# Two output-projection blocks begun in turn, and one step more ahead of a product, in a two-layer decoder trunk

## The chip, the core and the metric

The kernel runs on one core of a Trainium2 chip. The metric is device time in microseconds (us) of one execution, the median of three runs. The engines are named as in the profile: PE (TensorE, matmuls; PEld is its weight load), DVE (VectorE), ACT (ScalarE), POOL (GpSimd) and SP (SyncE, which here only issues DMAs).

## The reference

Two layers of a decoder trunk on one sequence of 256 tokens of width 2048, in float32. Each layer projects the normalised input to all heads at once, runs four groups of heads of width 512, gates each, and projects back onto the residual:

```python
h = rms_norm(x, norm_g)
p = split_columns(jnp.einsum("bsd,de->bse", h, w_in))
fox  = from_heads(forgetting_attention(...)) * jax.nn.silu(p["fox_g"])
diff = from_heads(rms_norm(differential_attention(...), diff_norm_g) * (1 - lambda_init)) * silu(p["diff_g"])
moba = from_heads(moba_attention(mq, mk, mv)) * jax.nn.silu(p["moba_g"])
gla  = from_heads(rms_norm(gla_chunked(...), gla_norm_g)) * jax.nn.silu(p["gla_g"])
mixed = jnp.concatenate([fox, diff, moba, gla], axis=-1)
return x + jnp.einsum("bse,ed->bsd", mixed, w_out)
```

With 256 tokens MoBA's blocks of 256 keys leave plain causal attention. After the second layer follows one more RMSNorm.

## The kernel before

**Matmuls.** Nearly all of PE's work is the two projections. For accuracy each weight and each activation is split into two fp32r parts, and three products are added: hi weights with the activation's high part, hi weights with its low part, lo weights with its high part. ACT makes `hi` from the loaded weights (`raw`), DVE makes `lo` as `raw - hi`. The activations, transposed, lie in `hTp` (the layer's normalised input, both parts) and in `mTh` and `mTl` (the mixed heads, high and low part), by k tiles of 128 rows. Four k tiles are a group, which for `mTh`/`mTl` is the output of one kind of heads: 0 forgetting, 1 differential, 2 MoBA, 3 linear attention.

**Steps.** `_blocks()` lists column blocks of `w_in` and `w_out`, `_steps()` cuts them into steps of two k tiles (four, where a block has some 260 columns) and sets their order; the weights lie in memory in that order. A block of 512 columns has eight steps of twelve matmuls (eight with hi, four with lo), which all add into one PSUM tile of the pool `mm` (two buffers). Blocks follow one another, except those with a `turn`: their steps alternate, a group of k tiles of each at a time. Before, only two or three blocks at the start of each layer's `w_in` had one. `w_out` has four blocks of 512 columns in each layer (the last cut in two in layer 1), and takes the groups in the order 3, 0, 1, 2, so that MoBA's is needed last.

**Order of the work.** The program is written out by a loop over the steps, in the order in which every engine then runs its part. For step i it emits: `hi` and `lo` of step i + 3 and the load of step i + 7 (`prepare`); what a finished block leaves to do (`settle`); the step's matmuls (`multiply`), for which the step's groups must have been emitted (`need`); and one round of `tick()`. Everything else, attention, linear attention, the next layer's input, is written as Python generators in the list `tasks`, and each round advances each of them to its next `yield`. So a `yield` is one step of distance. Where `need` isn't met, rounds are run without steps in between.

**The places that the change touches.**
- MoBA ends with `attend_columns`: PE makes p*v (`side<-pT,four`), DVE multiplies by the gate (`four<-side,gate`), `split_group` makes `mTh` on ACT and `mTl` on DVE.
- When a block of `w_out` is finished, `residual` puts it onto `xs` (ACT or DVE) and, in layer 0, starts `make_hT` for the chunk: for chunks 0 and 1 POOL adds x by DMA (L440); DVE transposes 32 x 32 squares (`four<-xs`); `moved` sends the tile to memory (L301, `turn<-four`) and, once that has landed, back in four DMAs in another order (L304, `four<-turn`); after `LAND` = 5 rounds `split_x` makes `hTp` on ACT and DVE. All of POOL's DMAs are issued in one order. Chunk 3 alone is transposed on PE (L281, `side<-ct,xs`).
- In `gla`, for each of two pairs of heads, ACT and DVE make the tile `ee` (`eight` in the profile) and `tq`; a `yield` stands between the last of that and the products of seven levels on PE (`side<-tq,eight`), which take both `side` tiles in PSUM.

Of the kernel before, what the change touches and what calls it, by code (L numbers as in the profile page):

```python
# [24 lines left out]
DEPTH = 2  # L25
# [70 lines left out]
def _blocks():  # L96

    def block(w, l, c0, n, kind, groups=(0, 1, 2, 3), turn=None):
        kts = [g * 4 + i for g in groups for i in range(4)]
        return {"w": w, "l": l, "c0": c0, "n": n, "kind": kind, "kts": kts, "per": 4 if n * 4 <= STEP_W else 2, "turn": turn}  # L100

    out = []
    for l in range(DEPTH):
        for i, (c0, n) in enumerate((
            (COL["gla_a"], 264),
            (COL["gla_q"], 512),
            (COL["gla_g"] + 248, 264),
            (COL["gla_v"], 512),
            (COL["fox_v"] + 258, 258),
            (COL["fox_q"], 512),  # L110
            (COL["fox_k"], 512),
            (COL["diff_q"], 512),
            (COL["diff_k"], 512),
            (COL["fox_v"], 258),
            (COL["fox_g"], 512),
            (COL["diff_v"], 512),
            (COL["moba_q"], 512),
            (COL["moba_k"], 512),
            (COL["diff_g"], 512),
            (COL["moba_g"], 512),  # L120
            (COL["moba_v"], 512),
        )):
            out.append(block("w_in", l, c0, n, "rows", turn=l if i in ((0, 1, 2), (0, 2))[l] else None))
        for chunk in range(4):
            cut = l + 1 == DEPTH and chunk == 3
            out.append(block("w_out", l, chunk * 512, 256 if cut else 512, "rows", (3, 0, 1, 2)))
    out.append(block("w_out", DEPTH - 1, D - 256, 256, "apart", (3, 0, 1, 2)))
    return out


def _steps():

    steps, first = [], {}
    for i, b in enumerate(_blocks()):
        per, turn = b["per"], b["turn"]
        for j in range(0, KT, per):
            key = (i, 0, 0) if turn is None else (first.setdefault(turn, i), j // 4, i)
            steps.append((key, len(steps), {"block": i, "kts": b["kts"][j:j + per], "first": j == 0, "last": j + per == KT}))
    steps = [s for _, _, s in sorted(steps, key=lambda z: z[:2])]
    at = 0  # L140
    for s in steps:
        s["at"] = at
        at += P * len(s["kts"]) * _BLOCKS[s["block"]]["n"]
    return steps
# [61 lines left out]
def hybrid_trunk(  # L206
# [405 lines left out]
    def gla(l, an):  # L612
        yield from until("constants")
        yield
        ps = yield from take_side()
        for m in range(2):
            transpose(ps[0:16, m * P:(m + 1) * P], an[:, m])
        yield
        v_.tensor_copy(at17[0:16], ps[0:16, 0:256])
        side.put(ps)  # L620
        yield
        al = yield from take_side()
        for pair in range(2):
            matmul(al[:, pair * SEQ:(pair + 1) * SEQ], wa[:, l, pair * P:(pair + 1) * P], at17, True, True)
        yield
        e = yield from s2.take([P, 512])
        gl = yield from s2.take([P, 2, SEQ])
        yield from log_sigmoid(gl.rearrange("p x t -> p (x t)"), al[:, :512], e)
        s2.put(e)
        side.put(al)  # L630
        yield
        cum = yield from s2.take([P, 2, SEQ])
        for pair in range(2):
            for m in range(2):
                c = slice(m * P, (m + 1) * P)
                v_.tensor_tensor_scan(cum[:, pair, c], gl[:, pair, c], gl[:, pair, c], 0.0, op0=OP.add, op1=OP.bypass)
        s2.put(gl)
        yield from until(("gla_qk", l))
        qkT = env["gla_qk", l].rearrange("p (a m) t -> p a (m t)", m=2)
        sT = yield from s4.take([P, 2, H, P])  # L640
        for m in range(2):
            for h in range(H):
                c = (h // 2 * 2 + m) * 2 + h % 2
                a_.activation(sT[:, m, h], ident, AF.Copy, scale=env["gla_dgs", l][:, c:c + 1])
            yield
        sx = yield from s2.take([P, H, P])
        for pair in range(2):
            ee = yield from s8.take([P, 2, NL + 1, P])
            for i, h in enumerate(GLA_LEVELS):
                src = cum[:, pair].rearrange("p (m b w) -> p m b w", m=2, w=2 * h)  # L650
                v_.tensor_sub(ee[:, :, i].rearrange("p m (b w) -> p m b w", w=2 * h), src,
                              src[:, :, :, h - 1:h].to_broadcast([P, 2, 64 // h, 2 * h]))
                if i == 3:
                    yield
            v_.tensor_scalar(ee[:, 0, NL], cum[:, pair, :P], cum[:, pair, P - 1:P], None, op0=OP.subtract)
            v_.tensor_copy(ee[:, 1, NL], cum[:, pair, P:])
            yield
            for m in range(2):
                a_.activation(ee[:, m], ee[:, m], AF.Abs)
                a_.activation(ee[:, m], ee[:, m], AF.Exp, scale=-1.0 / GLA_TAU)  # L660
                yield

            def half(z, h, second):
                return z.rearrange("p m (b two h) -> p m b two h", two=2, h=h)[:, :, :, second]

            qv = qkT[:, pair].rearrange("p (m t) -> p m t", m=2)
            kv = qkT[:, 2 + pair].rearrange("p (m t) -> p m t", m=2)
            for i, h in enumerate(GLA_LEVELS):
                for hh in range(2):
                    rows = slice(hh * 64, hh * 64 + 64)  # L670
                    v_.tensor_mul(tq[rows, :, i, hh].rearrange("p m (b h) -> p m b h", h=h), half(ee[rows, :, i], h, 1),
                                  half(qv[rows], h, 1))
                if i == 3:
                    yield
            yield
            for i, h in enumerate(GLA_LEVELS):
                dst = half(ee[:, :, i], h, 0)
                v_.tensor_mul(dst, dst, half(kv, h, 0))
            yield
            v_.tensor_mul(ee[:, 0, NL], ee[:, 0, NL], kv[:, 0])  # L680
            v_.tensor_mul(ee[:, 1, NL], ee[:, 1, NL], qv[:, 1])
            yield
            both = yield from take_both()
            pcs = [z.rearrange("p (l x c) -> p l x c", l=NL + 1, x=2) for z in both]
            for m in range(2):
                for i in range(NL):
                    matmul(pcs[m][:, i], ee[:, m, i], tq[:, m, i], True, True)
            for m in range(2):
                yield
                for i, h in enumerate(GLA_LEVELS):  # L690
                    dst = sT[:, m, pair * 2:pair * 2 + 2].rearrange("p x (b two h) -> p x b two h", two=2, h=h)[:, :, :, 1]
                    src = pcs[m][:, i].rearrange("p x (b h) -> p x b h", h=h)
                    mk = masks[:, i].rearrange("p (b h) -> p b h", h=h)[:, None].to_broadcast([P, 2, 64 // h, h])
                    v_.copy_predicated(dst, mk, src)
                side.put(both[m])
            px = yield from take_side()
            for hh in range(2):
                rows = slice(hh * 64, hh * 64 + 64)
                matmul(px[:, hh * 512:hh * 512 + P], ee[rows, 0, NL], ee[rows, 1, NL], True, True, tiles=2)
            s8.put(ee)  # L700
            yield
            a_.activation(sx[:, pair * 2:pair * 2 + 2], px.rearrange("p (h t) -> p h t", h=2)[:, :, :P], AF.Copy)
            side.put(px)
        s4.put(env["gla_qk", l])
        s2.put(cum)
        yield from until(("gla_v", l))
        yield
        vn = env["gla_v", l]
        ops = yield from take_side()
        o = ops.rearrange("p (m h d) -> p m h d", m=2, h=H)  # L710
        for h in range(H):
            matmul(o[:, 0, h], sT[:, 0, h], vn[:, 0, h * P:(h + 1) * P], True, True)
        for h in range(H):
            matmul(o[:, 1, h], sT[:, 1, h], vn[:, 1, h * P:(h + 1) * P], True, False)
            matmul(o[:, 1, h], sx[:, h], vn[:, 0, h * P:(h + 1) * P], False, True)
        s4.put(sT, vn)
        s2.put(sx)
        yield
        yield from finish_rows(l, 3, o, ops, None, env["gla_sg", l])
# [373 lines left out]
    for z in _BLOCKS:  # L1093
        l, f = next(dones)
# [233 lines left out]
```

## Time and profile before

| what | us |
|---|---|
| median of 3 runs (lowest to highest) | 926.46 (926.28 to 927.83) |
| the profiled execution | 925.78 |
| its span, first to last instruction | 924.0 |
| PE busy | 907.0 |
| DVE busy | 625.6 |
| ACT busy | 506.4 |
| POOL busy | 88.9 |
| mean granted clock of PE, share of full speed | 0.994 |

The profile is of one execution. A row of the timeline gives start and duration in us from the span's start, engine, line of the kernel, operation, what is written and read, and in brackets how long the engine was idle before and what ended that. Line 176 is a helper through which all of ACT's and DVE's work goes, and line 277 one for matmuls, so the tiles' names tell the place. Matmuls overlap in the pipeline: one of 512 columns is shown with 0.39 us while they follow each other faster than that. Each layer has its own rows: layer 0's `w_out` lies about from 365 to 460 us, layer 1's at the end.

### The profile page before, as it was taken

What the parts mean: (1) busy time and instruction counts of PE and PEld (TensorE: products, weight loads), DVE (VectorE), ACT (ScalarE), POOL (GpSimd) and SP (SyncE); (2) the same over time, 40 slices, a digit from 0 to 9 for tenths busy, and PEclk for the clock granted to TensorE, in tenths of its full rate; (3) what the DMA queues carried; (4) which work ended last, traced back from release to release, by engine and by line L of the source; (5) the groups of instructions that cost most, each with busy time, mean ns of one, the idle gap of its engine ahead of it and who ended that gap; (6) DMA issues with size and microseconds to landing.
All of it is one profiled execution on the core that took longest, in us unless ns stands there. A gap on an engine that the chain in (4) does not pass through costs nothing.

```text
span 924.0 us, 12695 instructions
## 1 busy us (share of the span) xinstructions
PE 907.0 (98%) x4694; PEld 771.5 (83%) x4694; DVE 625.6 (68%) x967; ACT 506.4 (55%) x712; POOL 88.9 (10%) x145
## 2 busy tenths in 40 slices
PE   9999999999999999899999999999999999998996
PEld 7989888898888888788898887888888888887886
DVE  7656777787569578556755549867975885694562
ACT  6576773374554466346656575743645545743441
POOL 1010002220001121001200100012110012110000
PEclk9999999999999999999999999999999999999999
DMA  8776557767657768578855845867776576694652
GB/s 320 245 241 190 182 176 260 248 204 229 209 177 230 228 189 235 170 202 261 289 178 164 256 150 178 242 190 247 225 232 178 167 243 207 203 290 147 201 160 92
DMA packets 56865, 194.84 MB, mean 211 GB/s; under 512 B 8001, under 2 KB 8289, under 8 KB 56802
## 3 DMA queue, kind: packets, MB, share of 16 engines
q1 hardware_dynamic: 46048, 164.20, 55.6%
q0 software_dynamic: 9264, 28.32, 10.8%
q10 hardware_dynamic: 1490, 1.51, 0.6%
q8 instruction: 37, 0.61, 0.3%
q14 instruction: 26, 0.21, 0.1%
HBM read 178.79 MB, written 15.20 MB: 210 GB/s over the span
## 4 chain that ended last, share of the span: by engine, by line
PE 95%; DVE 2%; ACT 1%; issue 1%; DMA 0%; POOLq 0%; POOL 0%; DVEq 0%; SPq 0%; ACTq 0%
PE mm L277 86%; PE side L277 9%; ACT eight L176 0%; DMA four<-in_xt 0%; DVE tq L176 0%; DVE lo L176 0%; ACT hi L176 0%; DVE mTl L176 0%; DVE four L176 0%; ACT mTh L176 0%; DVE xs L176 0%; ACT L176 0%; PE side L281 0%; DVE hTp L176 0%; POOLq L1324 0%
## 5 line engine op out<-in xcount | busy, mean ns | idle before, releaser
L176 DVE TENSOR_TENSOR lo<-raw,hi 128x1024 fp32r<-128x1024 f32 (+3 forms) x301 | 364.6, 1220 | 251.8 <-ACT hi L176 250.3
L176 ACT ACTIVATE hi<-raw 128x1024 fp32r<-128x1024 f32 (+3 forms) x301 | 317.1, 1059 | 362.3 <-PE mm L277 310.0
L277 PE MATMUL mm<-hi,hTp 128*128 128x512 f32 (+2 forms) x2048 | 465.1, 371 | 0.0
L277 PEld LDWEIGHTS mm<-hi,hTp 128*128 128x128 f32 x2048 | 358.3, 188 | 66.0 <-ACT hi L176 1.0
L277 PE MATMUL mm<-lo,hTp 128*128 128x512 f32 (+2 forms) x1024 | 249.8, 369 | 0.1
L277 PEld LDWEIGHTS mm<-lo,hTp 128*128 128x128 f32 x1024 | 181.1, 188 | 32.8 <-DVE lo L176 0.3
L277 PE MATMUL mm<-hi,mTh 128*128 128x512 f32 (+1 forms) x256 | 96.7, 382 | 4.8 <-ACT mTh L176 4.8
L277 PE MATMUL mm<-hi,mTl 128*128 128x512 f32 (+1 forms) x256 | 97.0, 383 | 1.5 <-DVE mTl L176 1.5
L277 PE MATMUL mm<-lo,mTh 128*128 128x512 f32 (+1 forms) x256 | 64.4, 376 | 0.0
L277 PEld LDWEIGHTS mm<-hi,mTh 128*128 128x128 f32 x256 | 49.0, 192 | 14.0 <-ACT mTh L176 5.2
L277 PEld LDWEIGHTS mm<-hi,mTl 128*128 128x128 f32 x256 | 49.2, 192 | 11.2 <-DVE mTl L176 2.1
L304 POOL DMA_DIRECT2D four<-turn x84 | 46.0, 553 | 102.2 <-DMA turn<-four 43.5
L277 PEld LDWEIGHTS mm<-lo,mTh 128*128 128x128 f32 x256 | 46.4, 189 | 8.9
L301 POOL DMA_DIRECT2D turn<-four x21 | 12.2, 582 | 407.9 <-DVE four L176 407.9
L176 DVE STREAM_TRANSPOSE pT<-four 32x128 f32<-32x128 f32 (+1 forms) x116 | 39.3, 350 | 1.0
L176 ACT ACTIVATE four<-mm,rstd 128x512 f32<-128x512 f32 (+2 forms) x56 | 33.6, 648 | 3.6 <-DVE fx L176 3.6
L176 ACT ACT_TABLE_LOAD x24 | 30.8, 1283 | 3.3 <-DVE an L176 3.0
L277 PEld LDWEIGHTS side<-four,four 128*128 128x128 f32 (+1 forms) x224 | 22.0, 190 | 2.3 <-issue 1.4
L277 PE MATMUL side<-four,four 128*128 128x128 f32 (+1 forms) x224 | 23.3, 277 | 0.0
L176 DVE STREAM_TRANSPOSE four<-four 128x1024 f32<-128x1024 f32 x18 | 22.4, 1245 | 0.3
L176 ACT ACTIVATE four<-side,nb 128x256 f32<-128x256 f32 (+1 forms) x48 | 20.5, 444 | 0.6 <-DVE nb L176 0.6
L176 DVE COPY_PREDICATED four<-masks,side 128x128 f32<-128x128 uint8 x56 | 19.0, 340 | 1.8
(145 smaller groups left out, 545.1 us busy)
## 6 DMA issues: line engine op xcount, KB each, us to landing
raw<-in_weights SPq DMA_DIRECT2D x272, 512.0 KB, 4.1
turn<-four POOLq DMA_DIRECT2D x21, 512.0 KB, 5.0
four<-turn POOLq DMA_DIRECT2D x84, 128.0 KB, 4.4
raw<-in_weights SPq DMA_DIRECT2D x16, 516.0 KB, 4.9
raw<-in_weights SPq DMA_DIRECT2D x15, 528.0 KB, 4.9
turn<-gate POOLq DMA_DIRECT2D x4, 512.0 KB, 4.8
gate<-turn POOLq DMA_DIRECT2D x16, 128.0 KB, 5.3
four<-in_xt SPq DMA_DIRECT2D x3, 512.0 KB, 7.1
```

The source lines that it names most:

```text
L176: return f(*args, **kw)
L277: t_.matmul(out, lhsT, rhs, start=start, stop=stop)
L301: g_.dma_start(via, t.rearrange("p c a b -> p c (a b)"))
L304: g_.dma_start(t[c * 32:(c + 1) * 32].rearrange("p q a b -> p q (a b)"), via[:, c].rearrange("(q i) e -> i q e", q=4))
```

## The change

```diff
@@ _blocks
-            out.append(block("w_in", l, c0, n, "rows", turn=l if i in ((0, 1, 2), (0, 2))[l] else None))
+            out.append(block("w_in", l, c0, n, "rows", turn=(l, (4, 8, 12)) if i in ((0, 1, 2), (0, 2))[l] else None))
         for chunk in range(4):
             cut = l + 1 == DEPTH and chunk == 3
-            out.append(block("w_out", l, chunk * 512, 256 if cut else 512, "rows", (3, 0, 1, 2)))
+            out.append(block("w_out", l, chunk * 512, 256 if cut else 512, "rows", (3, 0, 1, 2),
+                             turn=(DEPTH + l, (12,)) if chunk < 2 else None))
@@ _steps
-            key = (i, 0, 0) if turn is None else (first.setdefault(turn, i), j // 4, i)
+            key = (i, 0, 0) if turn is None else (first.setdefault(turn[0], i), sum(j >= c for c in turn[1]), i)
@@ gla, for each pair of heads
             v_.tensor_mul(ee[:, 0, NL], ee[:, 0, NL], kv[:, 0])
             v_.tensor_mul(ee[:, 1, NL], ee[:, 1, NL], qv[:, 1])
             yield
+            yield
             both = yield from take_both()
```

A turn now names the k tiles at which it passes to the next block. For `w_in` nothing changes by that. In `w_out` of each layer blocks 0 and 1 form a turn that passes at k tile 12 alone: six steps of block 0, six of block 1, then the last two of block 0 and the last two of block 1. MoBA's group is therefore needed first by the thirteenth step of `w_out` instead of the seventh, block 0 is finished after step 14 instead of 8, block 1 after 16 as before. In `gla` one more `yield` stands ahead of the products of the levels. The number of instructions of the computation stays.

ACT in `w_out` of layer 0, before, from MoBA's `mTh` to the first chunks of the next layer's input (`xs<-mm` copies a finished block, `two,parts<-xs` takes squares of a chunk, `hTp` is the chunk's transposed input):

```order
L176 ACTIVATE four_3312<-mm,rstd 128x512 x2
L176 ACTIVATE hi<-raw 128x1024 x6
L176 ACTIVATE mTh<-four_3442 128x1024
L176 ACTIVATE hi<-raw 128x1024 x2
L176 ACTIVATE xs<-mm 128x512 x2
L176 ACTIVATE hi<-raw 128x1024 x6
L176 ACTIVATE two_3610,parts<-xs 128x512
L176 ACTIVATE two_3612,parts<-xs 128x512
L176 ACTIVATE hi<-raw 128x1024 x2
L176 ACTIVATE xs<-mm 128x512 x2
L176 ACTIVATE hi<-raw 128x1024 x4
L176 ACTIVATE hTp<-four_3607,ngt 128x256 x4
```

And after:

```order
L177 ACTIVATE four_3312<-mm,rstd 128x512 x2
L177 ACTIVATE hi<-raw 128x1024 x9
L177 ACTIVATE mTh<-four_3491 128x1024
L177 ACTIVATE hi<-raw 128x1024 x5
L177 ACTIVATE xs<-mm 128x512 x2
L177 ACTIVATE hi<-raw 128x1024 x2
L177 ACTIVATE xs<-mm 128x512 x2
L177 ACTIVATE hi<-raw 128x1024 x4
L177 ACTIVATE two_3722,parts<-xs 128x512
L177 ACTIVATE two_3724,parts<-xs 128x512
```

`mTh` stands three steps later, block 0's copy six steps later, and block 1's copy comes two steps behind it instead of eight.

POOL between the layers, before (three chunks, each with its way through memory; x is added to chunks 0 and 1):

```order
L440 DMA xs<-in_x 128x2x512
L301 DMA turn_3614<-four_3607 128x1024
L304 DMA four_3607<-turn_3614 32x4x256 x4
L440 DMA xs<-in_x 128x2x512
L301 DMA turn_3783<-four_3776 128x1024
L304 DMA four_3776<-turn_3783 32x4x256 x4
L301 DMA turn_3853<-four_3846 128x1024
L304 DMA four_3846<-turn_3853 32x4x256 x4
```

And after:

```order
L441 DMA xs<-in_x 128x2x512 x2
L302 DMA turn_3726<-four_3719 128x1024
L305 DMA four_3719<-turn_3726 32x4x256 x4
L302 DMA turn_3775<-four_3768 128x1024
L305 DMA four_3768<-turn_3775 32x4x256 x4
L302 DMA turn_3845<-four_3838 128x1024
L305 DMA four_3838<-turn_3845 32x4x256 x4
```

Both additions of x now stand ahead of chunk 0's way through memory, and the three ways follow one another.

PE at the first pair's products of the levels in layer 1, before (`hi` and `lo` carry the number of the step's tile):

```order
L277 MATMUL mm_4739<-lo_4831,hTp_113 128x512 x4
L277 MATMUL side0_4917<-tq_94,eight0_4722 128x128 x7
L277 MATMUL side1_4918<-tq_94,eight0_4722 128x128 x7
L277 MATMUL mm_4946<-hi_4854,hTp_113 128x512 x8
L277 MATMUL mm_4946<-lo_4855,hTp_113 128x512 x4
```

And after:

```order
L278 MATMUL mm_4739<-lo_4831,hTp_113 128x512 x4
L278 MATMUL mm_4930<-hi_4854,hTp_113 128x512 x8
L278 MATMUL mm_4930<-lo_4855,hTp_113 128x512 x4
L278 MATMUL side0_4943<-tq_94,eight0_4722 128x128 x7
L278 MATMUL side1_4944<-tq_94,eight0_4722 128x128 x7
```

One more step of the projection stands ahead of the products. The second pair's stand two steps later than before, in both layers, since each pair has its own `yield`.

## The prediction

> **What bounds the kernel now.** I read the page first, for the shares. The program's span and the engines' busy times:
>
> ```profile
> span 924.0 us, 12695 instructions
> PE 907.0 (98%) x4694; PEld 771.5 (83%) x4694; DVE 625.6 (68%) x967; ACT 506.4 (55%) x712; POOL 88.9 (10%) x145
> ```
>
> PE is busy in 98% of the span and no work is added to or taken from it, so only PE's idle and slow time can move. The view of waits, of PE alone, lists all of it that other engines cause (total, times, longest):
>
> ```profile
> PE mm L277 <- ACT mTh L176: 4.8, 2, 2.4
> PE mm L277 <- DVE mTl L176: 1.5, 2, 0.8
> PE side L342 <- DVE four L337: 1.3, 1, 1.3
> PE side L277 <- DVE eight L176: 0.8, 1, 0.8
> ```
>
> The first two are one place, once in each layer; L342 is the start, which is not touched; the last is one product of the linear attention's levels. Next the timeline at the first place, in layer 0 (start, duration, engine, instruction, idle time ahead in brackets):
>
> ```profile
> 381.47 2.84 PE L277 MATMUL side<-pT,four 128*128 128x128 f32 x24
> 384.35 1.22 DVE L176 TENSOR_TENSOR four<-side,gate 128x1024 f32<-128x1024 f32 x1 [1.27 <-PE side L277]
> 385.60 1.06 ACT L176 ACTIVATE mTh<-four 128x1024 fp32r<-128x1024 f32 x1 [3.78 <-DVE four L176]
> 386.69 1.23 DVE L176 TENSOR_TENSOR mTl<-four,mTh 128x1024 fp32r<-128x1024 f32 x1 [1.12 <-ACT mTh L176]
> 386.71 0.51 PE L277 MATMUL mm<-hi,mTh 128*128 128x512 f32 x1 [2.40 <-ACT mTh L176]
> 387.97 0.80 PE L277 MATMUL mm<-hi,mTl 128*128 128x512 f32 x1 [0.76 <-DVE mTl L176]
> 388.56 0.63 PE L277 MATMUL mm<-hi,mTh 128*128 128x512 f32 x1
> 391.06 1.07 PE L277 MATMUL mm<-lo,mTh 128*128 128x512 f32 x4
> 391.97 0.39 PE L277 MATMUL mm<-hi,mTh 128*128 128x512 f32 x1
> 393.78 1.07 PE L277 MATMUL mm<-lo,mTh 128*128 128x512 f32 x4
> ```
>
> PE makes MoBA's p*v, then in a chain one after the other DVE gates it, ACT takes mTh and DVE mTl, while the seventh step of `w_out`, which needs both, stands next on PE. After the wait the matmuls run at 0.63 us instead of 0.39. The view of windows gives the reason (PE, PEld, DVE, ACT, POOL, then granted clock, DMA share, GB/s); the third row is the same place in layer 1, the last one the wait at the levels' products:
>
> ```profile
> 384.31:391.06 6.75, 3.59 (x8) 2.67 (x9) 2.45 (x2) 1.06 (x1) 0.00 (x0) 0.75 0.20 70
> 391.06:450.00 58.94, 58.94 (x262) 48.82 (x261) 35.80 (x34) 31.60 (x42) 8.68 (x13) 1.00 0.79 231
> 838.45:845.00 6.55, 3.39 (x8) 2.50 (x9) 2.45 (x2) 1.06 (x1) 0.00 (x0) 0.74 0.22 76
> 563.40:567.00 3.60, 3.53 (x30) 3.49 (x31) 3.60 (x11) 3.12 (x7) 0.00 (x0) 1.00 0.54 156
> ```
>
> The granted clock is 0.75 in the first stretch and 1.00 behind it: this stall costs its idle time and then some slow matmuls, while the short wait of the last row left the clock at 1.00.
>
> **The change part by part.** *The turn of w_out, the gain.* A step lasts 393.78 - 391.06 = 2.72 us, its eight hi matmuls 393.78 - 391.97 = 1.81. From the end of p*v, 384.31 (the first window's edge; the row's 2.84 ends in the pipeline), to the seventh step's first lo product are 6.75 us. So this stall costs 6.75 - 1.81 = 4.94 us: 3.16 idle and 1.8 of slow and cut-up matmuls. In layer 1:
>
> ```profile
> 835.61 2.84 PE L277 MATMUL side<-pT,four 128*128 128x128 f32 x24
> 845.12 1.09 PE L277 MATMUL mm<-lo,mTh 128*128 128x512 f32 x4
> ```
>
> p*v lasts 2.84 there too and ends at 838.45, so 845.12 - 838.45 - 1.81 = 4.86 us.
>
> After the change the group is first needed by the thirteenth step, and p*v stands behind the eighth. Then p*v ends at 384.31 + 2 x 2.72 = 389.75 and the thirteenth step begins 4 x 2.72 later, at 400.6. In between, the gating stands behind lo number 12, mTh behind hi 13 and mTl behind lo 14 (the order of DVE and ACT). Two rows from before, where the ninth step begins at 393.78 + 0.91 = 394.69, show when such an instruction comes:
>
> ```profile
> 394.99 1.06 ACT L176 ACTIVATE xs<-mm 128x512 f32<-128x512 f32 x2
> 395.12 1.23 DVE L176 TENSOR_TENSOR lo<-raw,hi 128x1024 fp32r<-128x1024 f32 x1 [1.50 <-ACT hi L176]
> ```
>
> The second is lo 12, done 1.7 us into the step three before its own. So lo 14 is done at 389.75 + 2 x 2.72 + 1.7 = 396.9 and mTl 1.23 later, at 398.1: 2.5 us ahead of its use. Both stalls go: -4.94 - 4.86 = -9.8. Two accumulators in turn need no third buffer: block 0's is copied out 0.3 to 1.4 us after its last step (the first of these rows), and block 2 takes its place two steps (5.4 us) after it.
>
> *What is late next.* Block 0 of `w_out` is now done six steps later and two steps ahead of block 1, so layer 1's chunks 0, 1 and 2 send their turns through DRAM close together, on POOL's one queue: out (L301), wait for its landing, four back (L304), and only then the next chunk's. Before, chunk 0's were over long before chunk 1's. POOL's rows of these three and ACT's and DVE's that end the stage:
>
> ```profile
> 414.98 0.60 POOL L301 DMA_DIRECT2D turn<-four  x1 [17.35 <-DVE four L176]
> 421.27 2.20 POOL L304 DMA_DIRECT2D four<-turn  x4 [5.69 <-PE mm L277]
> 437.17 0.60 POOL L301 DMA_DIRECT2D turn<-four  x1 [12.45 <-DVE four L176]
> 443.37 2.22 POOL L304 DMA_DIRECT2D four<-turn  x4 [5.61 <-DMA turn<-four]
> 445.58 0.56 POOL L301 DMA_DIRECT2D turn<-four  x1
> 453.58 2.19 POOL L304 DMA_DIRECT2D four<-turn  x4 [7.43 <-DMA turn<-four]
> 450.98 2.79 ACT L176 ACTIVATE hTp<-four,ngt 128x256 fp32r<-128x256 f32 x4 [1.49 <-DMA four<-turn]
> 458.84 2.88 ACT L176 ACTIVATE hTp<-four,ngt 128x256 fp32r<-128x256 f32 x4 [1.22 <-DMA four<-turn]
> 463.91 1.28 DVE L176 TENSOR_TENSOR xs<-mm,xs 128x512 f32<-128x512 f32 x2
> 465.80 1.04 PE L281 MATMUL side<-ct,xs 128*128 128x128 f32 x8
> ```
>
> On ACT chunk 2's hTp (458.84) stands ahead of the next hi, that hi ahead of its lo, and on DVE that lo ahead of chunk 3's residual (463.91), which PE's transposes of L281 read. The residual ends at 465.19, 6.35 after hTp began, and PE comes to it at 465.80: 0.6 us to spare. The change makes PE come 4.94 earlier, at 460.86, while the chain starts later: chunk 0's first turn goes out at 414.98 + 6 x 2.72 - 4.94 = 426.36.
>
> From there I add: turn to its four, 421.27 - 414.98 = 6.29; the four issues, 2.20; chunk 1's turn, which now leaves right behind another chunk's four as chunk 2's did before, 453.58 - 445.58 = 8.00; 2.20; chunk 2's turn 8.00; from its four to hTp, 458.84 - 453.58 = 5.26. That is 31.95, and hTp of chunk 2 starts at 458.3, where at the old distance to PE it would start at 458.84 - 4.94 = 453.9. The residual ends at 464.65, so PE waits 464.65 - 460.86 = 3.8 us, once, between the layers.
>
> Its ends: with every turn at 6.20 (443.37 - 437.17, with nothing ahead of it) the two are 3.6 shorter and the wait is 0.2. The slowest turn behind another four stands in layer 0:
>
> ```profile
> 178.38 0.56 POOL L301 DMA_DIRECT2D turn<-four  x1
> 187.46 2.18 POOL L304 DMA_DIRECT2D four<-turn  x4 [8.51 <-ACT hi L176]
> ```
>
> 9.08; two of them and a last landing of 7.61 (450.98 - 443.37) make it 4.5 longer: 8.3 us. I take 8.00, the row with the same neighbours at the same place. The x added by DMA (L440) is no part of it: both now leave ahead of the first turn, the second right after block 1's copy, at 394.99 + 1.06 + 8 x 2.72 - 4.94 = 412.9, and it lands in about 8.9 by the list of DMA issues, before chunk 1's transposes two steps behind 423:
>
> ```profile
> xs<-in_x POOLq DMA_DIRECT2D x2, 512.0 KB, 8.9
> ```
>
>
> To a wait of 3.8 comes the slow clock. Behind the wait of 2.40 and 0.76 the seven matmuls from 387.97 to 391.06 took 3.09 instead of 7/8 x 1.81 = 1.58, so 1.5; behind the 0.8 at the levels' products the clock was kept. 3.8 is nearer to the first: +1.5. [...]
>
> *The step more ahead of the levels' products.* It takes away the one wait of 0.8 in layer 1: products that stand one step (2.72) later find `eight` ready. It also moves the linear attention's end by two steps and with it the forgetting and differential attention's products by up to two. In the order, these stand in layer 0 after where they stood in layer 1 before, and the other way round, and neither place made PE wait in the list above, so I cost it at nothing; weights' hi and lo have three steps of lead for cover. Without that cover it would be a wait like the old 0.8. -0.8.
>
> Sum: -4.94 - 4.86 - 0.8 + 3.8 + 1.5 = -5.3. The profiled execution took 925.78 (span 924.0 and 1.8 around it), 0.7 below the median 926.46; -5.3 gives 920.5 against the first and 921.2 against the second. I say 920.7.
>
> **The rivals.** *No new wait* (0.28). The turns land faster when spread: while ACT is held, the weights' loads pause too. For it speaks that elsewhere a turn has come back in 609.44 - 605.72 = 3.72 us:
>
> ```profile
> 605.72 0.56 POOL L301 DMA_DIRECT2D turn<-four  x1 [23.88 <-DVE four L176]
> 609.44 2.19 POOL L304 DMA_DIRECT2D four<-turn  x4 [3.16 <-ACT hi L176]
> ```
>
> Two turns 1.9 shorter than 8.00 each already end the wait; then 926.1 - 10.6 = 915.5, taking the middle of both bases. Against it: all three turns of this place took 6.2 to 8.0. [...]
>
> *A long wait* (0.12): the chain at its upper end, 8.3 + 1.5, eats 9.8 of 10.6: 925.3.
>
> *Slower* (0.03): the same queue, with each of the three turns at 9.08 and each landing slow enough that hTp of chunk 2 starts later than 453.9 + 0.6 + 10.6 - 1.5, which is 463.6, or 37.2 us after the first turn instead of 31.95. From there every us is a loss; 41 us would give 930.
>
> *The change does not do what it says* (0.05): mTl misses the thirteenth step, because p*v, gating and mTl wait for their place behind hi and lo. It has 2.5 us to spare; if DVE is late by 4, then 1.5 per layer stay, each with 1.5 of slow clock, 2 x 3.0, and the time is 926.1 - 5.3 + 6.0 = 926.8.
>
> **How the numbers follow.** My forecast (a wait of 1.5 to 6 us between the layers, nothing else) has 0.52: 918 to 923. A measurement here cannot tell less than 0.2% (1.9 us) from no change. The range 915.3 to 924 holds the forecast and the first rival and leaves out the last three. Faster: 0.52 + 0.28, and 0.09 of the long wait and the half-kept stalls that stay below 924.6, 0.89; same 0.08; slower 0.03.
>
> **What would show it.** Right: no wait of PE for mTh or mTl, clock 1.00 there; one wait of PE's L281 for xs at about 461; ACT's hTp of chunks 1 and 2 idle 3 to 6 us each for four<-turn; POOL's turns at 8 us each, back to back from 426. Wrong: no wait at L281 (the transfers were faster), a wait at the thirteenth step, or one of `side` products in the attention stages, which I cost at nothing.

## The result, and the profile after

| | median, us | lowest to highest | executions |
|---|---|---|---|
| before | 926.46 | 926.00 to 928.33 | 7 |
| after | 915.55 | 914.54 to 922.53 | 7 |

The ratio is 0.9899, 95% interval 0.9866 to 0.9931: 10.9 us faster at the medians. The forecast was 920.7 with a range from 915.3 to 924.0, so the range holds it, but at its lower end, where the rival "No new wait" stood (915.5); the forecast by itself, 918 to 923, does not hold it. The executions of after do not lie round one value: five lie within 914.5 to 918.0 and two at 922.5. That spread is what most of the experiments are about.

The page of after, span and engines. PE has 4.3 us less of busy time for the same 4694 matmuls, the rest of the 10.3 us of span is idle time:

```profile
span 913.7 us, 12702 instructions
PE 902.7 (99%) x4694; PEld 769.4 (84%) x4694; DVE 625.6 (68%) x967; ACT 505.8 (55%) x712; POOL 89.1 (10%) x145
```

The view of waits of PE in after (total, times, longest). The waits for `mTh`, `mTl` and `eight` are gone; new are two short ones at the transposes of L282 (L281 in before). The one of 0.5 for `hTp` stands at the program's start, at 5.49 us, where the same matmuls began at 5.55 in before, so it costs nothing:

```profile
PE side L343 <- DVE four L338: 1.3, 1, 1.3
PE mm L278 <- DVE hTp L177: 0.5, 1, 0.5
PE side L282 <- PE side L278: 0.3, 1, 0.3
PE side L282 <- DVE xs L177: 0.2, 1, 0.2
```

The timeline of after at the place of the old stall in layer 0 (start, duration): MoBA's group, and the first matmul of the thirteenth step, which needs it first.

```profile
392.46 1.04 ACT L177 ACTIVATE mTh<-four 128x1024 fp32r<-128x1024 f32 x1
396.50 1.22 DVE L177 TENSOR_TENSOR mTl<-four,mTh 128x1024 fp32r<-128x1024 f32 x1
400.36 0.39 PE L278 MATMUL mm<-hi,mTh 128*128 128x512 f32 x1
```

`mTl` is done at 397.72, 2.6 us ahead of its use. The windows of before's two stalls, now of after (PE, PEld, DVE, ACT, POOL, granted clock, DMA share, GB/s), show PE busy throughout and the clock at 1.00 where it was 0.75 and 0.74:

```profile
384.31:391.06 6.75, 6.75 (x43) 6.05 (x42) 3.68 (x3) 1.17 (x2) 0.00 (x0) 1.00 0.68 207
838.45:845.00 6.55, 6.55 (x31) 5.45 (x30) 3.12 (x3) 3.07 (x3) 0.00 (x0) 1.00 0.38 118
```

Between the layers, the timeline of after: POOL's turns of layer 1's chunks 0, 1 and 2, ACT's `hTp` of chunks 1 and 2, DVE's residual of chunk 3 and PE's transposes of it.

```profile
426.10 0.57 POOL L302 DMA_DIRECT2D turn<-four  x1 [12.04 <-DVE four L177]
432.59 2.22 POOL L305 DMA_DIRECT2D four<-turn  x4 [5.92 <-PE mm L278]
434.81 0.57 POOL L302 DMA_DIRECT2D turn<-four  x1
442.60 2.23 POOL L305 DMA_DIRECT2D four<-turn  x4 [7.22 <-DMA turn<-four]
444.82 0.56 POOL L302 DMA_DIRECT2D turn<-four  x1
449.89 2.19 POOL L305 DMA_DIRECT2D four<-turn  x4 [4.51 <-DMA turn<-four]
448.22 2.85 ACT L177 ACTIVATE hTp<-four,ngt 128x256 fp32r<-128x256 f32 x4 [3.15 <-DMA four<-turn]
455.12 2.96 ACT L177 ACTIVATE hTp<-four,ngt 128x256 fp32r<-128x256 f32 x4 [1.12 <-DMA four<-turn]
460.27 1.28 DVE L177 TENSOR_TENSOR xs<-mm,xs 128x512 f32<-128x512 f32 x2
461.06 0.30 PE L282 MATMUL side<-ct,xs 128*128 128x128 f32 x1 [0.30 <-PE side L278]
461.61 0.98 PE L282 MATMUL side<-ct,xs 128*128 128x128 f32 x7 [0.25 <-DVE xs L177]
```

The queue does what the prediction says: one chunk's turn leaves right behind the four of the chunk before. Turn to four takes 6.49, 7.79 and 5.07 us, and from the last four to `hTp` it is 5.23. The whole chain, from the first turn to `hTp` of chunk 2, is 455.12 - 426.10 = 29.0 us, and PE waits 0.30 + 0.25 = 0.55 us.

### The profile page after: what moved, and what is told of

It reads as the page before. It is cut to its first block, busy times and chain, and to the rows that moved or that the text cites. A ratio compares the mean times of both kernels' runs of the same rounds, so it can differ in the third digit from the quotient of the medians.

```text
span 913.7 us, 12702 instructions
## 1 busy us (share of the span) xinstructions
PE 902.7 (99%) x4694; PEld 769.4 (84%) x4694; DVE 625.6 (68%) x967; ACT 505.8 (55%) x712; POOL 89.1 (10%) x145
## 4 chain that ended last, share of the span: by engine, by line
PE 98%; issue 1%; DVE 0%; DMA 0%; POOLq 0%; POOL 0%; ACT 0%; DVEq 0%; SPq 0%; ACTq 0%
PE mm L278 88%; PE side L278 9%; DMA four<-in_xt 0%; DVE xs L177 0%; PE side L282 0%; DVE hTp L177 0%; DVE lo L177 0%; POOLq L1326 0%; POOL rf L400 0%; ACT two L177 0%; DVEq L1326 0%; SPq L1110 0%; DVE ssf L177 0%; DVE pw L177 0%; DVEq L177 0%
## 5 line engine op out<-in xcount | busy, mean ns | idle before, releaser
L278 PE MATMUL mm<-hi,mTl 128*128 128x512 f32 (+1 forms) x256 | 95.0, 376 | 0.0
```

The source lines that it names most:

```text
L278: t_.matmul(out, lhsT, rhs, start=start, stop=stop)
```

## The experiments

Theory 1: the gain is the two stalls and the levels' wait, and the one new cost is the wait between the layers, whose size is set by how fast three turns come back one after the other on POOL's queue; this differs from execution to execution. Rival: the queue is no part of it; the longer executions lose their time elsewhere, or the stalls were worth less than counted.

**The changed kernel again, four times: `a1_after_again`, and three single executions.** No edit.

> The changed kernel again, to see how its runs spread. Its seven runs so far lay at 914.5 to 915.6 (four), 918.0 (one) and 922.5 (two). Theory 1 (the ways of chunks 0 to 2 through memory, one after the other on POOL's queue): the transfers' landing differs from run to run, and a run is slow when chunk 2's last one lands late. Then most runs lie at 914.5 to 916, some up to 923, and whenever the profiled run is a slow one, PE waits at the transposes of chunk 3 (L282) and the clock is at half behind it. Theory 2 (the levels' products moved): the slow runs come from the attention stages, where the order changed; a slow profile would show PE waiting at side products there and nothing at L282.

Measured: median 915.05 (914.37 to 923.17, 6 executions), ratio 0.9893 (0.9867 to 0.9918). Its profiled execution took 918.2: PE waits at L282, as expected, but the clock stays at 1.00 behind it, which was not.

> The changed kernel unaltered, one profiled execution, to learn what its longer runs are made of. Theory 1 (the third turn between the layers lands sooner or later from run to run): an execution near 915 has at most 0.5 us of wait at the transposes of xs (L282) and a full clock through the middle of the span; one at 918 has 2 to 3 us there and a full clock; one at 922 or more has 4 us or more there and one or two windows of half clock right behind it, 463 to 471. POOL's turn of chunk 2 to its four is under 6 us in the first, 6.5 to 7.5 in the second, 8 or more in the last. Rival (the longer runs lose time elsewhere: a loading transfer or an attention stage that is late): the span differs with the L282 wait unchanged, and another wait of PE is in the list.

> The same kernel once more, as the run before it. Theory 1: the span beyond 913 is the wait at L282 beyond 0.5 plus half of the time at half clock in mid span. Rival: the excess of the span stands at another line.

> The same kernel once more, as the two before it. Theory 1: the span beyond 913 is the wait at L282 beyond 0.5 plus half of the time at half clock in mid span. Rival: the excess of the span stands at another line.

Measured: 921.09, 914.66 and 915.30. The first of the three is one of the longer executions, with its profile. Its wait at L282 in the list of waits:

```profile
PE side L282 <- issue: 4.3, 1, 4.3
PE side L282 <- DVE xs L177: 0.2, 1, 0.2
```

And the timeline of the same execution, the rows of after above without `hTp` of chunk 1:

```profile
426.10 0.57 POOL L302 DMA_DIRECT2D turn<-four  x1 [12.04 <-DVE four L177]
432.03 2.22 POOL L305 DMA_DIRECT2D four<-turn  x4 [5.36 <-DMA turn<-four]
434.24 0.56 POOL L302 DMA_DIRECT2D turn<-four  x1
442.14 2.22 POOL L305 DMA_DIRECT2D four<-turn  x4 [7.33 <-DMA turn<-four]
444.35 0.56 POOL L302 DMA_DIRECT2D turn<-four  x1
451.85 2.19 POOL L305 DMA_DIRECT2D four<-turn  x4 [6.95 <-DMA turn<-four]
459.20 2.84 ACT L177 ACTIVATE hTp<-four,ngt 128x256 fp32r<-128x256 f32 x4 [5.01 <-DMA four<-turn]
464.22 1.28 DVE L177 TENSOR_TENSOR xs<-mm,xs 128x512 f32<-128x512 f32 x2
465.01 0.30 PE L282 MATMUL side<-ct,xs 128*128 128x128 f32 x1 [4.27 <-issue]
465.56 1.75 PE L282 MATMUL side<-ct,xs 128*128 128x128 f32 x7 [0.25 <-DVE xs L177]
```

Up to the third turn the two executions are within 0.6 us of one another. Then the turn takes 7.50 instead of 5.07 and the way back 7.35 instead of 5.23; `hTp` starts 4.1 us later and PE too (465.01 against 461.06). The wait's name, "issue", means that no released semaphore was matched to it; the residual's end, 465.50, and the next row's releaser tell what it was. The same chain in each profiled execution of the changed kernel:

| execution | three turns, us | last four to `hTp` | first turn to `hTp` | wait at L282 | half clock behind it | span |
|---|---|---|---|---|---|---|
| after | 6.49, 7.79, 5.07 | 5.23 | 29.0 | 0.55 | 0 | 913.7 |
| a1 | 6.07, 8.47, 6.81 | 5.57 | 31.3 | 2.87 | 0 | 916.4 |
| a2 | 5.93, 7.90, 7.50 | 7.35 | 33.1 | 4.52 | 3.41 | 919.3 |
| a3 | 5.67, 5.66, 6.81 | 4.79 | 27.3 | 0 | 0 | 912.9 |
| a4 | 3.82, 7.52, 7.93 | 4.56 | 28.3 | 0 | 0 | 913.5 |

(The time from one chunk's four to the next chunk's turn, 2.2, makes up the rest of the sum.) By the prediction's own step the residual ends 6.35 after `hTp` and PE comes at 460.86, so the wait should begin at a chain of 460.86 - 6.35 - 426.1 = 28.4 us and grow one for one. That gives 0.6, 2.9 and 4.7 for the first three and nothing for the last two; measured are 0.55, 2.87, 4.52, 0 and 0. The span follows: a2 less a3 is 6.4, of which 4.52 is the wait and 1.7 the stretch of 3.41 us at half clock behind it. Theory 1 holds and the rival falls for these five. One sign named beforehand failed: chunk 2's turn alone was to tell the executions apart, under 6 us in the short ones, and it took 6.81 and 7.93 in a3 and a4, which do not wait. It is the whole chain that counts. Of all sixteen executions of the changed kernel ten lie within 914.37 and 915.55, two at 918 and four within 921.1 and 923.2; the three above 922 have no profile, and that they are the same thing is argued from their size.

**One part alone.** `e1_yield_only` keeps the additional step ahead of the levels' products and takes the turn back:

```diff
-                             turn=(DEPTH + l, (12,)) if chunk < 2 else None))
+                             turn=None))
```

> Only the extra step ahead of the levels' products; w_out as before. Theory 1: PE loses the wait at these products in layer 1 alone, 0.8 to 1.0 us, and the two stalls of 4.9 us at mTh and mTl stay: 925.4 to 925.8 against 926.5, no runs above 929. Rival (the changed order of attention makes slow runs): some runs 3 to 8 us above the others.

Measured: 926.07 (12 executions, 924.15 to 932.59) against 927.12 of before (23 executions, 924.06 to 930.21), ratio 0.9997 (0.9981 to 1.0014): no difference that can be told. The execution at 932.59 is above the 929 that theory 1 allowed; it has no profile and is unexplained, so for this kernel the rival is not ruled out (before itself reaches 930.21). Its waits:

```profile
PE mm L278 <- ACT mTh L177: 4.8, 2, 2.4
PE mm L278 <- DVE mTl L177: 1.5, 2, 0.8
PE side L343 <- DVE four L338: 1.3, 1, 1.3
```

Both stalls are there, the wait for `eight` is gone, and the span is 923.6 against 924.0. `e2_turn_only` is the opposite:

```diff
             v_.tensor_mul(ee[:, 1, NL], ee[:, 1, NL], qv[:, 1])
             yield
-            yield
```

> Only the turn of the two blocks of w_out, without the extra step ahead of the levels' products. Both theories: the two stalls of 4.9 us go, the wait of 0.8 to 1.0 at the levels' products in layer 1 stays, so the faster runs lie at 915.5 to 916.5. Theory 1: slow runs up to 923 as with the whole change. Theory 2: no slow runs, all within 1.5 us of each other.

Measured: 916.22 (915.37 to 916.73, 4 executions), ratio 0.9887 (0.9874 to 0.9899). In its waits stands again

```profile
PE side L278 <- DVE eight L177: 0.8, 1, 0.8
```

So the step more takes away the wait of 0.8 that it was costed at, seen in the profiles from both sides; the times agree (916.22 against 915.05 for the whole change), but cannot resolve it. In e2's profile the chain was 27.3 us, there was no wait at L282, and the span of 913.6 is 0.7 above a3's. All four executions lie within 1.4 us of each other, which was the sign of theory 2 (the levels' products) and not of theory 1. With ten short ones in sixteen, four short ones in a row come about once in seven times (0.625 to the fourth is 0.15), so this does not decide between them; the profiles of a1 and a2 do, with the lost time at L282 and no wait at the levels' products.

**One layer alone.** `e3_layer0_only` and `e4_layer1_only`:

```diff
-                             turn=(DEPTH + l, (12,)) if chunk < 2 else None))
+                             turn=(DEPTH + l, (12,)) if chunk < 2 and l == 0 else None))
```

(and `l == 1` in the other).

> The whole change, but the turn of the two blocks only in layer 0's w_out. Theory 1: layer 0's stall (4.94) and the products' wait (about 0.9) go, layer 1's stall of 4.86 stays; the new wait between the layers is there: 920 to 921 in most runs, some up to 928. Rival: the slow runs have nothing to do with layer 0's turn, and would be as frequent in the next kernel as in this one.

> The whole change, but the turn only in layer 1's w_out. Theory 1: layer 1's stall (4.86) and the products' wait go, layer 0's stall of 4.94 stays, and chunk 0's way through memory is over long before chunk 1's as before: 920.5 to 921.3, with no run more than 2.5 us above the median and no wait at L282. Rival: slow runs as in the one before.

Measured, against 927.12: layer 0 alone 921.83 (919.91 to 927.25, 12 executions), ratio 0.9950 (0.9931 to 0.9969); layer 1 alone 920.29 (919.90 to 924.18, 6 executions), ratio 0.9937 (0.9914 to 0.9959). Each keeps the other layer's stall. Layer 1 alone has the place between the layers as before; its span is 918.6, 5.4 less than before, where the stall of layer 1 and the levels' wait were costed at 4.86 + 0.8 = 5.7. Two things were expected otherwise: a wait of 0.2 stands at L282, and one execution, without a profile, lies 3.9 above the median instead of at most 2.5. Before's own 23 executions spread over 6.2 us, so not every longer execution is explained by the turn of layer 0. Layer 0 alone has a span of 920.5, 3.5 less: 4.94 + 0.8 less a wait of 0.7 at L282 (a chain of 29.2 us), and the stall left in layer 1 cost it two stretches of 3.41 us at half clock where before's cost one, 1.7 more; that makes 3.3. Both gains are clear of the noise and of about the size counted, and the two parts add up to the whole: 5.3 and 6.8 at the medians, less the step's 1.05 that both contain, make 11.1, against 11.6 for a1 and its own before (926.64). The 1.05 is itself within e1's noise.

**The suspected queue made longer: `e6_chunk2_twice`.** One further transfer of chunk 2's tile to memory is put ahead of its turn on POOL's queue; nobody reads it.

```diff
         squares(l, chunk, parts)
+        if l == 1 and chunk == 2:
+            spare = dram.tile([P, 4, 256], F32, name="spare", tag="spare", bufs=1)
+            g_.dma_start(spare, t.rearrange("p c a b -> p c (a b)"))
         yield from moved(t)
```

> The whole change, and chunk 2 of layer 1's input is sent to memory once more, to a spare place, just ahead of its own turn: the queue is made longer by one transfer of 512 KB, nothing else changes. Theory 1: chunk 2's input comes 3 to 5 us later, PE waits 3 to 5 us at L282 and runs at half clock for one or two stretches of 3.4 us behind it: 919 to 922 in nearly every run, like the slow runs of the changed kernel. Theory 2: the queue does not matter, 914.5 to 916 with the same share of slow runs.

Measured: 925.17 (920.60 to 926.96, 12 executions), ratio 0.9973 (0.9958 to 0.9988). One 512 KB transfer that nobody reads takes back nearly the whole gain, more than expected: nine of the twelve are above 922. The timeline of its profiled execution (span 921.1):

```profile
442.45 0.56 POOL L462 DMA_DIRECT2D spare<-four  x1
443.05 0.56 POOL L302 DMA_DIRECT2D turn<-four  x1
452.42 2.21 POOL L305 DMA_DIRECT2D four<-turn  x4 [8.82 <-issue]
465.75 2.31 PE L282 MATMUL side<-ct,xs 128*128 128x128 f32 x8 [4.89 <-issue]
```

The turn behind it takes 9.37, the chain 33.8, PE waits 4.89 and has two stretches of 3.41 us at half speed. The four have to wait for the additional transfer as well, since they overwrite the tile that it reads; the 8.82 of idle time ahead of them is named "issue", so the row does not tell which of the two transfers ended it. The span is 8.2 above a3's, of which the wait is 4.89, the two half-speed stretches 2.5 (they hold 1.9 of the wait) and a wait of 0.6 at a later product the most of the rest. So a longer queue between the layers costs the gain: in the profile at L282 and in the clock behind it; for the eleven others that is argued from their times, none of which is below 920.60. The median is near the 925.3 of the rival "A long wait", but that rival's wait of 8.3 is not shown by any profile.

**The queue begun sooner: `e5_ways_sooner`.** In `make_hT` of layer 1, the turns of chunks 0 and 1 are sent two steps and one step earlier, which the change allows since x is added long before:

```diff
             c = slice(chunk * 512, chunk * 512 + 512)
-            yield
             g_.dma_start(xs[:, :, c], x[0, :, c].rearrange("(m p) c -> p m c", p=P), accum_op=OP.add)
-            for _ in range(4):
+            for _ in range((3, 4)[chunk]):
                 yield
```

> The whole change, and layer 1's chunks 0 and 1 start their way through memory sooner: one round less ahead of the addition of x, and one less behind it for chunk 0. Chunk 0's first turn leaves at about 420.7 us instead of 426.1, chunk 1's at about 429 instead of 434.8, chunk 2's at about 440 instead of 444.8. Theory 1: some 4.8 us more room before chunk 3's transposes, so the slow runs go: median 914.5 to 915.2, all runs within 1.5 us, no wait at L282. Theory 2: slow runs up to 922 stay.

> The kernel whose chunks start their way through memory sooner, again, for more runs beside the thirteen of the changed kernel, of which five were 918 or more. Theory 1: all runs at 914.3 to 915.5. Rival: about four in ten at 918 or more.

Measured: 914.66 (914.45 to 914.91, 4 executions), ratio 0.9872 (0.9857 to 0.9886), and again 915.20 (914.68 to 916.22, 4 executions), ratio 0.9873 (0.9850 to 0.9896). All eight executions are at or below 916.22, where six of sixteen of the changed kernel lie at about 918 or above. The first profile, from chunk 2's turn on:

```profile
441.73 0.56 POOL L302 DMA_DIRECT2D turn<-four  x1 [3.47 <-DVE four L177]
446.19 2.18 POOL L305 DMA_DIRECT2D four<-turn  x4 [3.90 <-DMA turn<-four]
453.76 2.96 ACT L177 ACTIVATE hTp<-four,ngt 128x256 fp32r<-128x256 f32 x4 [1.40 <-DMA four<-turn]
460.53 1.04 PE L282 MATMUL side<-ct,xs 128*128 128x128 f32 x8
```

The turns now leave when DVE has made the tile, not when the queue comes free, and chunk 2's is back at 446.19 instead of 449.89. But the way back took 7.57 here, and `hTp` at 453.76 (454.31 in the second) is only 0.7 and 0.2 ahead of the 454.5 from which PE would wait, where 4.8 us more room was expected; a3, without the edit, has it at 453.54. So the profiles show no more room than in the quick executions of the changed kernel, and that the longer executions are gone rests on eight times alone, of which two are above the 915.5 expected. The medians, 914.66 and 915.20, cannot be told from the 915.05 of a1.

## Why the prediction was right, and where its size was off

- *The stalls, -4.94 and -4.86.* Right. No wait and clock 1.00 at both; `mTl` is done at 397.72 (predicted 398.1) and the thirteenth step begins at 400.36 (400.6). The single layers give 5.4 and 3.5 where the same terms, with what else those kernels hold, make 5.7 and 3.3.
- *The levels' products, -0.8.* Right by the waits of e1 and e2, too small for the times. The other `side` products of the attention stages, which were costed at nothing, show no wait in four of the five profiles of the changed kernel; a4 has one of 0.53, at 569.48, for `four`.
- *The place of the new wait and its chain.* Right in after: POOL's first turn at 426.10 (426.36), chunk 1's at 434.81 (434.85 by the sum), chunk 2's at 444.82 (445.05), though at 441.94 and 441.82 in a3 and a4; 6.35 from `hTp` to the residual's end came out as 6.43 and 6.30, and PE came at 461.06 less 0.30.
- *The wait, +3.8.* This step failed in its size. The mis-sized term is the chain of 31.95, and what was too long in it differs: in after chunk 2's turn (5.07 instead of 8.00), in a3 chunk 1's (5.66 instead of 8.00) and chunk 2's (6.81), in a4 chunk 0's (3.82 instead of 6.29). I took one execution's durations for fixed numbers, and "the row with the same neighbours at the same place" for the best price. In after the third turn took 5.07, and over the five profiles the three turns are 3.8 to 8.5 us and the chain 27.3 to 33.1, with my 31.95 near its upper end. The wait is therefore 0 to 0.6 in the common execution and 2.9 to 4.5 in others. The forecast's mechanism, a wait of 1.5 to 6, is seen in a1 and a2 (918.2 and 921.09, beside the forecast 920.7); the median is of the rival "No new wait". Ten of the sixteen executions went the rival's way and six the forecast's, against chances of 0.28 and 0.52. That the measured time lies in the range is owed to the range's having been drawn to hold that rival too; that the median execution was a short one is luck as far as this prediction goes. The spread could have been seen: before's own rows held turns of 3.72 to 9.08, which with the other terms (2.20 twice and 5.26) make chains of 20.8 to 36.9, and the 28.4 at which the wait begins lies inside.
- *The signs.* In after `hTp` of chunks 1 and 2 waited 3.15 and 1.12 for `four<-turn`, where 3 to 6 each were named, and the turns took 5.07 to 7.79, where 8 each were named. These speak for the rival; a1 and a2 are nearer to the signs named.
- *The slow clock, +1.5.* It is no fixed price of a wait: 0 at 2.87 in a1, and one stretch of 3.41 us at half clock, 1.7, at 4.52 in a2. The next but one section has the stretches that were measured.
- *The sum.* With the terms that held, -4.94 - 4.86 - 0.8, a3, which has no wait at all, should have a span of 913.4; it has 912.9.
- *The rivals.* "Change does not do what it says" fell with `mTl` 2.6 us early; "A long wait" and "Slower" did not occur in sixteen executions.

Open is why the same 512 KB come back after 4.5 us in one execution and after 7 in another. The load beside them does not tell it: the windows of after's third turn and, below it, of a2's (the share of the DMA engines and GB/s are the last two columns) show the quick turn with the busier engines:

```profile
445.00:450.00 5.00, 5.00 (x23) 4.13 (x22) 2.48 (x4) 1.85 (x4) 0.49 (x2) 1.00 0.92 304
```

```profile
445.00:452.00 7.00, 7.00 (x32) 5.82 (x31) 3.68 (x5) 3.58 (x5) 0.15 (x1) 1.00 0.82 270
```

The shortest turn of the table is a4's first, 3.82 us to the next issue; the other fourteen took 5.07 to 8.47.

## What to carry to other kernels

When a change makes several round trips through memory follow each other on one in-order queue, price the chain as a spread, from all rows of that transfer (here 3.8 to 8.5 us for one trip out), and compare the spread with the time at which the reader comes: the answer is a chance, not a sum. If the threshold lies inside the spread, it is worth trying to send the trips off as soon as their data is there rather than at the distance that suited the old order; here eight executions are in favour and the room gained in the profiles is not. And an experiment that lengthens the suspected queue by one transfer that nobody reads shows quickly whether time is lost there.

## What the runs showed of the hardware

Up to its last matmul the granted clock of before is 0.50 from 387.55 to 390.97 us and from 841.53 to 844.94, 3.41 us each time, and 1.00 on both sides. The windows of the 3.41 us ahead of the first of these, at the old stall, and of the stretch itself (the first value after the length is PE's busy time, the third from the end the granted clock):

```profile
384.14:387.55 3.41, 0.67 (x3) 0.19 (x1) 2.08 (x2) 1.06 (x1) 0.00 (x0) 1.00 0.48 144
387.55:390.97 3.42, 3.00 (x7) 2.43 (x8) 0.37 (x1) 0.00 (x0) 0.00 (x0) 0.50 0.02 5
```

a1, in two stretches of that length laid so that they share its wait of 2.87; the clock stayed at 1.00:

```profile
459.14:462.55 3.41, 1.97 (x17) 1.76 (x15) 3.12 (x5) 3.41 (x5) 0.00 (x0) 1.00 0.54 203
462.55:465.96 3.41, 1.99 (x16) 1.83 (x17) 3.41 (x5) 1.79 (x4) 0.00 (x0) 1.00 0.52 156
```

a2, where a wait of 4.52 left PE 0.31 of busy time in the 3.41 us ahead of the half clock:

```profile
458.75:462.16 3.41, 1.99 (x17) 1.78 (x15) 2.11 (x4) 2.96 (x5) 0.00 (x0) 1.00 0.56 229
462.16:465.57 3.41, 0.31 (x2) 0.15 (x2) 3.12 (x5) 2.80 (x3) 0.00 (x0) 1.00 0.14 17
465.57:468.98 3.41, 3.41 (x16) 3.41 (x17) 2.30 (x3) 1.57 (x4) 0.00 (x0) 0.50 0.72 218
```

In layer 1 of before PE was busy for 0.84 of the 3.42 us ahead of the half clock (838.11 to 841.53), in e3 for 1.34 of 3.41 (832.41 to 835.82). So 2.74 us of idle time in such a stretch of before (0.67 of 3.41 busy) and 2.07 in the one of e3 were followed by half clock. PE's share in a stretch does not tell it alone: counted from 459.80, a1 too has 3.41 us with PE busy for 1.31, and the clock was 1.00 there and in the 3.42 behind it. What decides it is not shown.

Nearly the same stall (2.40 and 0.76 in before, 2.4 and 0.5 in e3) cost one stretch of 3.41 us at half clock in before's layer 1 and two in e3's, 835.82 to 842.65. In the first of them PE was busy for 83% in before (2.83 of 3.41) and for 77% in e3 (2.63 of 3.42); why a second followed in e3 alone is not shown.
